# HGRN2 chain steps between projection matmuls: one step at each place, or two steps at every second place

## The chip, the cores and the metric

One core of a Trainium2 chip runs the kernel. The metric is device time in microseconds (us) of one execution. PE is TensorE (matmul), DVE is VectorE, ACT is ScalarE, POOL is GpSimd, SP issues the transfers.

## The reference, cut to what matters

One step of a streaming encoder with one layer. All 2048 new frames of a prompt (and 8 x 16 frames of running streams) go through one input projection to eight groups of 512 columns. Four of them (QA, KA, VA, GA) feed a stick-breaking attention with 8 heads, four (QH, FH, IH, GH) an HGRN2 recurrence with 4 heads of 128 x 128 state. An output projection and a layer norm follow. The change concerns the time in which the projection and the recurrence run together. The recurrence, per head:

```
f = lb + (1.0 - lb) * sigmoid(fh);  k = 1 - f;  q = silu(qh)
S_t = diag(f_t) S_{t-1} + k_t outer i_t
o_t = S_t^T q_t
o   = o * rsqrt(mean(o * o) + eps) * norm_g * silu(gh)
```

## The kernel before, in words

Everything is float32; projections are split in a high and a low part, so each product is three matmuls (lines 306 to 324). The order of the instructions is written out by hand: every engine runs its own instructions in the order in which the program issues them, and waits on semaphores where one needs another's result.

**Projection.** `order` (lines 222 to 231) lists the weight sections in two halves of the frames. In each half, head by head: IH (for two heads, ahead of heads 0 and 2), FH, QH, GH of the head, then 3, 3, 2 and 6 attention sections: KA0, QA0, VA0 after head 0; GA0, VA2, KA1 after head 1; QA1, GA1 after head 2; KA2, QA2, GA2, KA3, QA3, GA3 after head 3. A half has three tiles of tokens, of 384 columns (the last of the second half has 256; the last of the first half holds 256 prompt frames and the 128 frames of the running streams). For a narrow section a tile is one group of 24 matmuls into `pj` (`pe_T`, two buffers), with a gap after k = 2, after k = 5 and at its end, behind the evacuation (`evac_T`). VA and IH (wide sections) go by blocks of 128 tokens with two gaps per block (`pe_N`). At each gap `weave` is called (line 583). Evacuations: FH is a sigmoid on ACT (L337) and a tensor_scalar on DVE (L338); QH, GH and GA are a sigmoid on ACT (L327) and a product on DVE (L329, L331); QA, KA, VA are copies on ACT. After the first tile of a section (line 657) the next section's weights are split by `split_w`: casts on ACT (L107), subtractions on POOL (L115), two for a narrow section and four for a wide one.

**Recurrence.** After a head's GH section, its three tiles of tokens are appended to the list `chains` as three generators `hgrn` (line 393), which share the head's state. One call of `next` is one step. A chain has 14 steps:

- S (lines 405 to 412): kS = 1 - f, dp = q kS, q = q f, on DVE (L405, L411, L412); no matmul.
- seven levels 1, 2, 4, 8, 16, 32, 64 (lines 417 to 455): matmuls of kS and q into `ps` (two buffers): L418, six instructions, for levels 1 to 16; for levels 32 and 64 L431, with 32 or 64 columns into part of the output partitions. Then DVE rescales q (L443) and kS (L444), which the next level's matmuls read, keeps the scores (L435 or L438) and makes the next `tot` (L447). ACT and POOL make dh and dl at levels 2 and 4.
- K (lines 456 to 470): L457 and L458, the transposes of kS (L462), their copy kN on ACT (L464).
- U (471 to 486): pu = kN x i (L474), then the states on DVE (L484).
- O (487 to 501): po (L489, L491; L496 for the running streams), squares on ACT (L500).
- R (502 to 504): the reciprocal root on POOL (L129, L130).
- N (505 to 507): on = po x rs on DVE (L506), into a tile of one buffer.
- Q (508 to 516): transposes of `on` (L510), the gated product on DVE (L511), the store.

The third chain of a head in the first half holds the running streams and has two more steps: I, a product on POOL (L520), and B, its matmuls and state (L525, L527).

**The mixing.** `step_chain` (line 563) takes the first chain of the list, runs one step, and puts it back at the second place, so that the first two chains alternate and the third comes when one of them is done. `weave` adds the rate 1.0 to a credit, up to 2.0, and runs a step for each whole credit. `drain` (line 590) runs a chain to its end where a section needs its buffers.

Of the kernel before, what the change touches and what calls it, by code (L numbers as in the profile page):

```python
# [39 lines left out]
PASSES = ((0, 8), (8, 12), (12, 16))  # L40
NP = H // 2
HRATE = 1.0
SRATE = 0.9
CRATE = 2
ORATE = 0.9
# [20 lines left out]
def stream_step_kernel(ctx: ExitStack, tc: tile.TileContext, x_prompt, x_sample, cache_k, cache_v, state_s,  # L66
# [55 lines left out]
    def tick():  # L122
        for d in late:
            d[0] -= 1
        while late and late[0][0] <= 0:
            late.pop(0)[1]()
# [67 lines left out]
    with ExitStack() as ph:  # L194
# [366 lines left out]
        credit = [0.0]  # L561

        def step_chain():
            if not chains:
                return False
            g = chains.pop(0)
            done = next(g[1], 0) == 0
            if not done:
                chains.insert(min(1, len(chains)), g)
            return True  # L570

        RATE = HRATE

        prep = []

        def run_prep(n):
            while prep and n:
                if next(prep[0], 0) == 0:
                    prep.pop(0)
                else:  # L580
                    n -= 1

        def weave(rate):
            tick()
            run_prep(1)
            credit[0] = min(credit[0] + rate, 2.0)
            while credit[0] >= 1.0 and step_chain():
                credit[0] -= 1.0

        def drain(upto):  # L590
            while any(c[0] <= upto for c in chains):
# [18 lines left out]
        for i, (half, sec, j) in enumerate(order):  # L610
# [22 lines left out]
            for ti, (t0, n) in enumerate(TILES[half]):  # L633
                if wide(sec):
                    for b in range(n // P):
                        ps = pp.tile([P, 512], F32, name="pj", tag="pj")
                        o = ps[:, :256]
                        for _ in pe_N(ti, o, b, w):
                            weave(RATE)
                        evac_N(half, sec, j, ti, b, o, hg)  # L640
                        weave(RATE)
                else:
                    ps = pp.tile([P, 512], F32, name="pj", tag="pj")
                    o = ps[:, :n]
                    for _ in pe_T(ti, o, n, w):
                        weave(RATE)
                    if i == 1 and ti == 0:
                        next(consts, None)
                    for a in pend:
                        k_natural(*a)  # L650
                    pend = []
                    kn = evac_T(half, sec, j, ti, o, n, hg)
                    if kn:
                        pend.append(kn)
                    weave(RATE)
                if ti == (i == 0):
                    split_w(i + 1)
                elif ti == 1 and i + 2 < len(order):
                    load_raw(first_load[i + 2] + 2)
                if last:  # L660
                    prep.append(gen1(prep_x(1, ti)))
# [11 lines left out]
    with ExitStack() as ph:  # L673
# [318 lines left out]
        credit = [0.0]  # L992
# [7 lines left out]
        def run_steps(n0, n1, guest, rate):  # L1000
            for n in range(n0, n1):
                for fn in todo.pop(n, []):
                    fn()
                for i in range(2):
                    run_later()
                    s_part(n + LS, i)
                    if 0 <= n < NU:
                        t_part(n, i)
                    if i == 1:
                        z_part(n + LZ)  # L1010
                        c_part(n - 1)
                    tick()
                    if n >= -LZ:
                        credit[0] += rate
                    while credit[0] >= 1:
                        next(guest, None)
                        credit[0] -= 1
# [37 lines left out]
        credit[0] = C0  # L1055
        run_steps(0, NS, guest, SRATE)
        for _ in guest:
# [218 lines left out]
```

## Time and profile before

| what | value |
|---|---|
| runs of the kernel | median 1751.0 us of 3 (1747.85 to 1751.8) |
| the profiled execution | 1749.85 us |
| its span, first to last instruction | 1748.0 us |
| PE busy | 1707.1 us (98% of the span) |
| DVE, ACT, POOL busy | 958.5, 701.2, 731.2 us |
| the chain of work that ended last | 92% of it on PE |

The projections and the recurrence fill the first 990 us or so; attention, the running streams and the output projection follow. Rows of a timeline give the start and the duration in us, the engine, the line of the kernel, the operation, output<-inputs, shapes and how many instructions are merged (x6); in brackets the idle time before it and what ended it. Durations of matmuls reach into the next one: their ends are modelled.

### The profile page before, as it was taken

The numbers are of one execution on the slowest core, as the hardware profiler recorded it, in microseconds if no ns is written. First come the engines' busy times: TensorE is split into PE (matmuls) and PEld (weight loads), VectorE is DVE, ScalarE is ACT, GpSimd is POOL, SyncE is SP. The second block draws the span as 40 slices with busy tenths as digits, with TensorE's granted clock in tenths as the row PEclk, the third lists the DMA queues.
The fourth block names the chain that finished last, engine by engine and source line by source line (L and its number), as shares of the span: only waits on it lengthen the run. The fifth ranks groups of instructions, "written<-read, shape, count | busy, mean of one in ns | idle before, by whom it ended". The sixth has DMA issues, their size and how long they took to land.

```text
span 1748.0 us, 33628 instructions
## 1 busy us (share of the span) xinstructions
PE 1707.1 (98%) x12901; PEld 1464.1 (84%) x12901; DVE 958.5 (55%) x1762; ACT 701.2 (40%) x1593; POOL 731.2 (42%) x822
## 2 busy tenths in 40 slices
PE   8999999999999999999999999999999999999998
PEld 8999999999999999999999866666666667666886
DVE  4254543355443352642665367777877767666454
ACT  3221220212213222211222267777777877767210
POOL 1122321213221322221222266666766776766564
PEclk9999999999999999999999989999999999999999
DMA  4133232122244231231122476786644533131243
GB/s 166 53 89 102 63 100 61 48 63 62 81 120 135 62 103 56 80 90 40 61 62 76 124 189 159 176 187 152 152 113 136 185 114 102 53 114 40 92 147 115
DMA packets 288167, 180.01 MB, mean 103 GB/s; under 512 B 112636, under 2 KB 272904, under 8 KB 288008
## 3 DMA queue, kind: packets, MB, share of 16 engines
q1 hardware_dynamic: 288008, 177.86, 35.9%
q8 instruction: 103, 1.69, 0.4%
q14 instruction: 56, 0.46, 0.1%
HBM read 130.63 MB, written 47.71 MB: 102 GB/s over the span
## 4 chain that ended last, share of the span: by engine, by line
PE 92%; DVE 3%; ACT 1%; DMA 1%; issue 1%; SPq 1%; POOL 0%; POOLq 0%; DVEq 0%; ACTq 0%
PE pj L309 11%; PE pj L311 10%; PE pj L310 10%; PE z L734 9%; PE po L783 7%; PE wt L767 7%; PE py L1109 4%; PE ps L418 4%; PE pj L319 4%; PE pj L321 4%; PE pj L320 4%; PE py L1111 4%; PE py L1110 4%; PE pk L864 2%; PE so L945 1%; PE ps L431 1%
## 5 line engine op out<-in xcount | busy, mean ns | idle before, releaser
L115 POOL TENSOR_TENSOR wl<-wr,wh 128x512 fp32r<-128x512 f32 x126 | 163.8, 1322 | 578.7 <-ACT wh L107 561.0
L309 PE MATMUL pj<-xh,wh 128*128 128x384 f32 (+1 forms) x1152 | 395.5, 343 | 0.0
L754 POOL TENSOR_TENSOR s<-s,pr 128x512 f32<-128x512 f32 (+3 forms) x320 | 325.7, 1024 | 130.0 <-DVE pr L701 112.8
L311 PE MATMUL pj<-xh,wl 128*128 128x384 f32 (+1 forms) x1152 | 376.2, 327 | 0.0
L310 PE MATMUL pj<-xl,wh 128*128 128x384 f32 (+1 forms) x1152 | 375.8, 326 | 0.0
L701 DVE TENSOR_TENSOR_SCAN pr<-keep,pr,one 128x513 f32<-128x513 f32 x192 | 238.7, 1270 | 74.1 <-ACT keep L740 67.5
L309 PEld LDWEIGHTS pj<-xh,wh 128*128 128x128 f32 x1152 | 217.3, 189 | 2.7 <-issue 0.7
L310 PEld LDWEIGHTS pj<-xl,wh 128*128 128x128 f32 x1152 | 217.5, 189 | 0.7 <-issue 0.7
L311 PEld LDWEIGHTS pj<-xh,wl 128*128 128x128 f32 x1152 | 216.7, 188 | 0.0
L783 PEld LDWEIGHTS po<-wh,vst 128*64 128x64 f32 x2176 | 116.3, 137 | 100.6 <-issue 82.3
L737 ACT ACTIVATE s<-z 128x512 f32<-128x512 f32 (+3 forms) x320 | 173.4, 542 | 61.4 <-PE z L734 57.8
L107 ACT COPY wh<-wt 128x512 f32<-128x512 f32 (+3 forms) x320 | 165.6, 539 | 78.2 <-PE wt L767 65.1
L767 PE MATMUL wt<-ident,s 128*128 128x128 f32 x1088 | 171.5, 282 | 0.2
L734 PE MATMUL z<-kst,qr 64*128 64x512 f32 (+3 forms) x640 | 170.5, 587 | 0.1
L767 PEld LDWEIGHTS wt<-ident,s 128*128 128x128 f32 x1088 | 124.0, 142 | 45.2 <-issue 19.1
L319 PE MATMUL pj<-wh,xh 128*128 128x256 f32 x544 | 160.4, 295 | 0.0
L783 PE MATMUL po<-wh,vst 128*64 128x128 f32 x2176 | 155.0, 281 | 0.0
L320 PE MATMUL pj<-wl,xh 128*128 128x256 f32 x544 | 152.3, 280 | 0.3 <-POOL wl L115 0.3
L321 PE MATMUL pj<-wh,xl 128*128 128x256 f32 x544 | 152.2, 280 | 0.0
L327 ACT ACTIVATE sg<-pj 128x384 f32<-128x384 f32 (+1 forms) x72 | 34.1, 474 | 231.3 <-PE pj L311 217.9
L740 ACT ACTIVATE keep<-z 128x512 f32<-128x512 f32 (+2 forms) x230 | 126.0, 548 | 0.0
L701 DVE TENSOR_TENSOR_SCAN pr<-keep,one 128x385 f32<-128x385 f32 (+3 forms) x124 | 99.7, 820 | 33.2 <-ACT keep L740 17.6
(162 smaller groups left out, 2783.8 us busy)
## 6 DMA issues: line engine op xcount, KB each, us to landing
wr<-in_w_in SPq DMA_DIRECT2D x64, 512.0 KB
kr<-in_cache_k SPq DMA_DIRECT2D x16, 1024.0 KB
vr<-in_cache_v SPq DMA_DIRECT2D x32, 512.0 KB
mt<-mx_d SPq DMA_DIRECT2D x136, 64.0 KB
x<-in_x_prompt SPq DMA_DIRECT2D x16, 512.0 KB
kst<-kT_d SPq DMA_DIRECT2D x16, 512.0 KB
vst<-v_d SPq DMA_DIRECT2D x16, 512.0 KB
out<-xr SPq DMA_DIRECT2D x16, 512.0 KB
```

The source lines that it names most:

```text
L309: mm(o, wh[:, k], xh[:, k, :n], start=k == 0, stop=False)
L310: mm(o, wh[:, k], xl[:, k, :n], start=False, stop=False)
L311: mm(o, wl[:, k], xh[:, k, :n], start=False, stop=k == KT - 1)
L319: mm(o, xh[:, k, ts], wh[:, k], start=k == 0, stop=False)
L320: mm(o, xh[:, k, ts], wl[:, k], start=False, stop=False)
L321: mm(o, xl[:, k, ts], wh[:, k], start=False, stop=k == KT - 1)
L701: dve.tensor_tensor_scan(pr[:, CW - wd:CW + 1][:, ::-1], kr, by, carry, ALU.mult, ALU.bypass)
L734: mm(z[:, :wd], q[r, q0:q0 + P], k[r, lo:hi], start=not top, stop=True, skip_group_check=True)
L737: act.activation(s[:, :wd], z[:, :wd], AF.Sigmoid, scale=SC)
L754: pool.tensor_tensor(s[:, :wd], s[:, :wd], pr[:, CW - wd + 1:CW + 1], ALU.mult)
L767: nc.tensor.transpose(pt_[:, x:x + P], U[(u, a)][0][:, x:x + P], ident)
L783: mm(o[r, :P], v[:, lo // P + x, r], th[a][:, x * P:(x + 1) * P], start=top and x == 0, stop=bot and x == n - 1)
```

## The change

A constant HB = 2 is added. `weave` still counts a credit of 1.0 per call, now up to 4.0, and runs steps only when the credit has reached HB; then it runs as many as the credit pays for. Nothing else is changed.

```diff
+HB = 2
...
         def weave(rate):
             tick()
             run_prep(1)
-            credit[0] = min(credit[0] + rate, 2.0)
-            while credit[0] >= 1.0 and step_chain():
-                credit[0] -= 1.0
+            credit[0] = min(credit[0] + rate, 4.0)
+            if credit[0] >= HB:
+                while credit[0] >= 1.0 and step_chain():
+                    credit[0] -= 1.0
```

## Rows read from the trace of the kernel before

**Rows 1.** Windows: us, busy us (instructions) by engine, granted clock, DMA share, GB/s.
```profile
60.00:980.00 920.00, 908.09 (x6520) 885.58 (x6519) 417.81 (x1092) 197.19 (x514) 228.73 (x256) 1.00 0.26 76
```
**Rows 2.** Waits of PE, 60 to 980 us: total us, times, longest.
```profile
PE ps L418 <- DVE kS L444: 6.7, 9, 1.3
PE ps L418 <- DVE sc L435: 2.6, 2, 1.3
```
**Rows 3.** Timeline of PE, 253 to 264 us, two steps of one chain.
```profile
253.25 0.83 PE L418 MATMUL ps<-hq,kS 128*128 128x128 f32 x6
...
260.91 0.91 PE L418 MATMUL ps<-hq,kS 128*128 128x128 f32 x6 [1.30 <-DVE kS L444]
```
**Rows 4.** Timeline of DVE, the same stretch.
```profile
254.40 0.35 DVE L444 TENSOR_TENSOR kS<-kS,hf 128x192 f32<-128x192 f32 x1
...
259.35 1.42 DVE L444 TENSOR_TENSOR kS<-kS,tot 128x192 f32<-128x192 f32 x1
```
**Rows 5.** Timeline of PE, the end of GH of head 1.
```profile
195.07 0.33 PE L309 MATMUL pj<-xh,wh 128*128 128x384 f32 x1
...
197.15 0.33 PE L309 MATMUL pj<-xh,wh 128*128 128x384 f32 x1
```
**Rows 6.** Timeline of DVE, the two steps S that open head 1.
```profile
196.31 0.62 DVE L331 SCALAR_TENSOR_TENSOR hg<-pj,vecs,sg 128x384 f32<-128x384 f32 x1 [3.54 <-ACT sg L327]
...
...
197.83 0.56 DVE L412 TENSOR_TENSOR hq<-hq,hf 128x384 f32<-128x384 f32 x1
...
199.28 0.56 DVE L412 TENSOR_TENSOR hq<-hq,hf 128x384 f32<-128x384 f32 x1
```
**Rows 7.** Timeline of PE, a step of level 32.
```profile
105.41 0.47 PE L431 MATMUL ps<-hq,kS 128*32 128x32 f32 x12
```
**Rows 8.** Timeline of DVE, the same step.
```profile
106.18 0.35 DVE L444 TENSOR_TENSOR kS<-kS,tot 128x192 f32<-128x192 f32 x1
```
**Rows 9.** Timeline of PE, the transposes of a step K.
```profile
114.01 0.49 PE L462 MATMUL pk<-ident,kS 128*128 128x128 f32 x3
```
**Rows 10.** Timeline of ACT, the copy of the same step.
```profile
114.59 0.48 ACT L464 COPY kN<-pk 128x384 f32<-128x384 f32 x1 [2.47 <-PE pk L462]
```
**Rows 11.** Timeline of PE, the end of a step O with running streams.
```profile
157.43 1.95 PE L496 MATMUL po<-s,qz 128*128 128x128 f32 x16
```
**Rows 12.** Timeline of DVE, step N of the same chain.
```profile
161.56 0.56 DVE L506 TENSOR_TENSOR on<-po,rs 128x384 f32<-128x384 f32 x1
```
**Rows 13.** Timeline of ACT, the evacuation of an FH group.
```profile
314.19 0.49 ACT L337 ACTIVATE hf<-pj 128x384 f32<-128x384 f32 x1 [3.67 <-PE pj L311]
```
**Rows 14.** Timeline of DVE, the same evacuation.
```profile
314.72 0.48 DVE L338 TENSOR_SCALAR hf<-hf,oml,lb 128x384 f32<-128x384 f32 x1 [3.68 <-ACT hf L337]
```
**Rows 15.** Timeline of POOL, two weight splits and step I.
```profile
161.53 2.54 POOL L115 TENSOR_TENSOR wl<-wr,wh 128x512 fp32r<-128x512 f32 x2
164.03 1.90 POOL L520 TENSOR_TENSOR qz<-hi,hmask 128x1024 f32<-128x1024 f32 x1
```
**Rows 16.** Timeline of PE, step Q of the first of two chains.
```profile
132.69 0.49 PE L510 MATMUL pq<-ident,on 128*128 128x128 f32 x3
```
**Rows 17.** Timeline of DVE, step N of the second chain.
```profile
133.39 0.56 DVE L506 TENSOR_TENSOR on<-po,rs 128x384 f32<-128x384 f32 x1 [7.54 <-ACT vt L381]
```
**Rows 18.** Timeline of PE, a step of level 64 between projections.
```profile
111.22 0.34 PE L311 MATMUL pj<-xh,wl 128*128 128x384 f32 x1
111.49 0.56 PE L431 MATMUL ps<-hq,kS 128*64 128x64 f32 x6
...
112.27 0.34 PE L310 MATMUL pj<-xl,wh 128*128 128x384 f32 x1
```
**Rows 19.** Windows, granted clock in the seventh number group (columns as in rows 1).
```profile
530.00:540.00 10.00, 8.36 (x63) 8.08 (x62) 4.12 (x7) 2.89 (x6) 0.12 (x1) 1.00 0.83 277
...
1036.00:1038.00 2.00, 0.56 (x5) 0.56 (x6) 2.00 (x3) 0.00 (x0) 1.41 (x2) 1.00 0.73 223
1038.00:1042.00 4.00, 4.00 (x29) 3.38 (x28) 2.69 (x5) 1.81 (x6) 2.58 (x5) 0.61 1.07 277
```

## The prediction

> **What bounds the kernel now.** I read the windows over the projection stage first. From 60 to 980 us TensorE is busy 908.09 of 920.00 us at a granted clock of 1.00; DVE is busy 418, ACT 197, POOL 229 [rows 1]. The change reorders work in this stage alone, and here every microsecond in which TensorE waits is added to the end. Next the list of waits of TensorE: in the whole stage it waits 6.7 us in 9 cases for L444 and 2.6 us in 2 for L435, both of the chains' steps on DVE [rows 2]. So the chains are hidden almost completely, and the reason is their spacing: the reader is to see that the waits are few and not longer than 1.3 us. Last I read the timeline at single places, for what a step needs from the one ahead of it.
>
> **Recurrence of a chain.** A level step's six matmuls start at 253.25 [rows 3]. DVE then rescales q (L443) and kS (L444, from 254.40 for 0.35 us) [rows 4], so the result stands at 254.75. From the end of an L444 to the matmuls that waited for it goes 0.14 us: 259.35 + 1.42 = 260.77, start 260.91 [rows 3, 4]. The next level of the same chain can thus start 254.89 - 253.25 = 1.64 us after the first. The six matmuls themselves hold TensorE 0.67 us (0.83 shown, of which the following matmul overlaps 0.16). Two levels of one chain behind each other leave TensorE idle 0.97 us, and the group after a wait took 0.91 instead of 0.83 [rows 3]: **1.05 us**. In the kernel before a third of a projection group, six or nine matmuls (1.04 to 1.56 us at 0.173, below), always stands between, which is why it is nearly free.
>
> **What the change does to the order.** I followed the list `chains` through all 568 weaves. Steps stay 344, in the same order, and none is left for a drain. Before, 336 places hold steps, one each (8 hold two). After, there are 164: 96 hold one step of each of two chains, 8 hold four, and **60 hold two steps of the same chain**. `step_chain` alternates among the first two chains, but each head has three, so the third runs alone, and its two steps lie behind each other with no projection between.
>
> **The terms**, for eight head groups (four heads, two halves):
>
> 1. *Opening, 8 groups.* The list is empty when a head's chains arrive, so the credit stands at its cap: 2 before (S, S), 4 now (S, S, 1, 1). The first place is at 197.15, nine projection matmuls after the head's last group ended; twelve take 2.08 us from 195.07, so 0.173 each [rows 5]. On DVE the gate evacuation (L331) ends at 196.93, the first S (its last operation is L412) at 197.83 + 0.56 = 198.39, the second at 199.84 [rows 6]. The first level step could start at 198.53 instead of 197.15 (wait 1.38), end at 199.20, and the second at 199.98 (wait 0.78). 2.2 us each: **+17.6**.
> 2. *Pairs (2, 4) and (8, 16) of the third chain*, 16 places; some have two blocks of tokens and less work, so 1.0: **+16**. In six of the eight (8, 16) the weight splits (L115 on POOL) run beside it and L443 or L444 takes 1.42 instead of 0.35 [rows 4]: one or two such, 8.6 more; but before waits there already (most of the 9.3 in rows 2, I take 6.5): **+2**.
> 3. *(32, 64)*, 8 places: level 32 starts at 105.41 and shows 0.47, so it holds TensorE to about 105.75 [rows 7]; L444 ends at 106.53 [rows 8]; plus 0.14: 0.95 us, and twice the two stand behind an evacuation on DVE (0.65): **+9**.
> 4. *(K, U)*, 8 places: the transposes start at 114.01 and hold TensorE to 114.34 [rows 9], the copy of kN on ACT ends at 115.07 [rows 10], plus 0.14: 0.87, with the slow start 0.95: **+7.6**.
> 5. *(O, R)*: R is on POOL alone, nothing. *(N, Q)*, 8 places: from the last matmul of O (157.43 + 1.95 - 0.16 = 159.22 [rows 11]) to the end of N (161.56 + 0.56 [rows 12]) and on to Q go 3.0 us; two weaves cover 2.6 to 2.8. 0.3 in five cases. In three the place is the end of a group, and N queues behind its evacuation, which ends on DVE 1.2 us after the last matmul [rows 13, 14]; then 0.56, 0.14 and the slow start: 2.0. **+7.5**.
> 6. *(S, 1)* of the third chain: in heads 2 and 3 of both halves it stands at the end of a group (FH or GA), where S queues on DVE behind the evacuation. ACT starts 0.2 us after the last matmul (314.19 [rows 13]), L338 ends at 315.20 [rows 14], S takes 1.46 (196.93 to 198.39 [rows 6]): 315.20 + 1.46 + 0.14 less 313.99 is 2.8, with the slow start 2.9 us of waiting, and an estimated 2.45 in the second half, where the third chain has two blocks for three: **+10.7**. Elsewhere DVE runs S ahead: nothing.
> 7. *(I, B)*, four places. I is 1.90 us on POOL, behind two splits of 2.54 us [rows 15] that begin some 1.3 us after a section's first tile, so it ends 5.7 us after it. B stands 3.9 us after that tile in head 3 (wait 1.9) and, since term 5 has held TensorE, 5.4 in heads 0 and 2 (wait 0.4 each); in head 1 no split is near. **+2.7**.
> 8. *(Q, Q) of the first two chains*, 8 places: `on` has one buffer, so the second N waits for the first Q (132.69 to 133.39), runs 0.56 to 133.95 [rows 16, 17], and the second Q can start at 134.09, when TensorE has been free since 133.02: 1.07. Before, a weave lay between. **+9**.
> 9. *Two chains under the splits*. DVE now gets two steps at once. Where four splits stand (ahead of a wide section, 1.3 to 6.5 us after the tile), two operations of 1.42 for each chain [rows 4] let the second chain's next matmuls start some 7.1 us after the tile; they are due at 5.1, so 2.0 us, where the kernel before waited up to 1.3 [rows 2]: 0.7 in head 1, and 1.4 at level 64 in head 0, in both halves. **+4**, between 0, if the splits fall between the steps, and 14, if every group's first two sections are hit.
> 10. *What is won.* Levels 32 and 64 write part of the output partitions, and from the projection ahead (111.22) to the second behind (112.27) go 1.05 us [rows 18]; two projections are 0.35, six matmuls 0.40 (0.56 shown less 0.23, over five gaps, is 0.066 each). 0.30 us is the change of shape. 24 such places fall away: **-7**. Around ordinary steps the same sum leaves 0.006 us: nothing.
>
> Sum: 17.6 + 16 + 2 + 9 + 7.6 + 7.5 + 10.7 + 2.7 + 9 + 4 - 7 = **+79 us**. Against the profiled execution's 1749.85 us that is 1829; the median of the runs stands 1.15 higher, so I say **1830**. At nothing I cost the half of the steps that come one weave later, with their stores (SP) and the load of the state, which is needed five places, or ten weaves, later; dl on POOL has three places; and the projection's evacuations that stand behind a waiting N on DVE, since `pj` has two buffers. If those covers fail, evacuations are late and TensorE waits at the next group.
>
> **The clock.** It stayed at 1.00 over 530 to 540 with TensorE busy 8.36 of 10 us, but after a stretch with 0.56 busy of 2.00 it fell to the lower level, 1.2 GHz, for most of the next 4 us, whose mean is 0.61 [rows 19]; that costs 0.39 x 4 = 1.6 us. The waits of terms 2 and 6 that reach 2.5 to 3 us could do the same.
>
> **Rivals.**
> - *The clock falls* at some eight of the long waits: 8 x 1.6 = 13 more, **1843**. For it: rows 19; against: the stage before kept 1.00 throughout, and dense projections follow each wait at once. The Trainium skill, TensorE: Matmul & The Clock Gate (Why this matters for your kernels), asks for no idle gaps between bursts of matmuls, as the array falls back to half its clock; by that rule this case would be the likelier. The trace bears it out only for a stretch nearly empty.
> - *It does what its words say*, always one step of each chain: terms 1, 8, 9 and 10 stay, +24, **1774**. The list with three chains speaks against it.
> - *Faster*: DVE, ACT and POOL are idle half of the stage, and if they had every next step ready, only term 10 were left: 1749.85 - 7, **1743**. It decides if a pair costs under 7 / 156 = 0.045 us per place. Against it stand 1.64 us of recurrence and in-order waiting [rows 2, 3].
> - *No change*: as many waits as term 10 gives back, at some seven places alone, 1751; it needs the same readiness as the case before.
>
> **How the numbers follow.** Forecast 0.73, clock 0.16, words 0.04, faster 0.04, no change 0.03. Low bounds of the terms (opening 13, pairs of 2 at 14 and -2, 6, 6.5, 4, 8, 0, 7, 0, -7) sum to about 49, so 1799; high ones (20, 18, 8, 11, 9, 12, 13, 8, 10, 10, -5) to 114, which with everything high at once is too much; I take 1857, which holds most of the clock's case. A measurement here tells 0.2% (3.5 us) from no change: faster 0.04, same 0.03, slower 0.93.
>
> **What would show it.** In the changed trace: TensorE's waits in the stage near 90 us instead of 10, in some 60 to 70 cases; at third-chain places two L418 groups 1.6 us apart with L444 as releaser; a wait for L412 at each head's opening; a wait of L510 for L506 of about 1 us; kN by ACT ahead of L474. The busy times of DVE, ACT and POOL stay. I am wrong if the third chain's level steps follow without a wait, or if the waits come but the stage after ends as early as now.

## The result, and the profile after

The changed kernel takes **1831.85 us** in the median of 4 runs (1829.49 to 1837.48), the kernel before 1749.42 us in 4 runs on the same chip (1747.16 to 1751.8). The ratio is 1.0474, 95% interval 1.0453 to 1.0495: slower by 82 us. The forecast said 1830, in 1799 to 1857.

The profiled run took 1837.48 us, its span 1835.6 us. The engines' busy times on the page of the changed kernel:

```profile
PE 1731.1 (94%) x12901; PEld 1482.1 (81%) x12901; DVE 950.3 (52%) x1762; ACT 701.4 (38%) x1593; POOL 730.9 (40%) x822
```

The work is the same (12901 matmuls, and DVE, ACT and POOL within 8.2 us of before); TensorE's busy time has grown by 24 us. Some 11 of it is the model of matmul ends (a matmul with a wait behind it is shown 0.16 us longer than it holds TensorE, and there are some 70 waits); the rest, some 13 us, fits the slower clock shown below. The last projection matmul ends at 994.0 us before and at 1078.9 us now, +84.9 us; what follows it took 754.0 us and now 756.7, with the clock at its lower level for 6.8 us more. So nearly all of the loss is in the projection stage, as the prediction had it. (1.9 us of the 84.9 stand ahead of it: in the profiled run the first matmul of L310 starts at 45.0 us, its counterpart L309 before at 43.1.) The windows of the changed kernel over that stage:

```profile
60.00:1065.00 1005.00, 930.11 (x6532) 901.81 (x6531) 409.93 (x1092) 197.67 (x515) 227.61 (x256) 0.98 0.24 70
```

Beside [rows 1], TensorE is busy 930 us instead of 908, for 12 matmuls more, and is idle 75 instead of 12; the clock's mean is 0.98 instead of 1.00. Two things, then: waits, and a clock. First the waits of PE in the changed kernel, from 60 to 1070 us:

```profile
PE ps L419 <- DVE hq L413: 21.7, 20, 2.6
PE ps L419 <- DVE kS L445: 19.0, 16, 2.0
PE pq L511 <- DVE on L507: 11.2, 11, 1.8
PE ps L432 <- DVE kS L445: 7.0, 8, 1.4
PE pu L475 <- ACT kN L465: 4.1, 8, 0.6
PE ps L458 <- DVE tot L448: 3.3, 2, 1.8
PE ps L419 <- DVE sc L436: 3.1, 2, 1.6
PE pb L526 <- POOL qz L521: 2.6, 2, 2.4
...
PE ps L419 <- DVE tot L448: 1.0, 4, 0.4
```

(The numbers of lines behind the inserted constant are one or two higher.) Where [rows 2] had 9.3 us in 11 cases, there are 73 us in 73. The four largest kinds of releaser are the prediction's: L413 for S, L445 for the chain's own rescaling, L507 for N, L465 for kN. One place of each kind shows the size. Two levels of a third chain, timelines of PE and of DVE in the changed kernel:

```profile
146.32 0.83 PE L419 MATMUL ps<-hq,kS 128*128 128x128 f32 x6
147.96 0.91 PE L419 MATMUL ps<-hq,kS 128*128 128x128 f32 x6 [0.81 <-DVE kS L445]
```

```profile
147.19 0.36 DVE L444 TENSOR_TENSOR hq<-hq,tot 128x192 f32<-128x192 f32 x1 [2.03 <-PE ps L419]
147.46 0.35 DVE L445 TENSOR_TENSOR kS<-kS,tot 128x192 f32<-128x192 f32 x1
```

The two groups start 1.64 us apart, as worked out ahead. The opening of head 0, PE and DVE of the changed kernel:

```profile
85.65 0.93 PE L419 MATMUL ps<-hq,kS 128*128 128x128 f32 x6 [1.12 <-DVE hq L413]
87.10 0.94 PE L419 MATMUL ps<-hq,kS 128*128 128x128 f32 x6 [0.52 <-DVE hq L413]
```

```profile
85.04 0.56 DVE L413 TENSOR_TENSOR hq<-hq,hf 128x384 f32<-128x384 f32 x1
...
86.49 0.56 DVE L413 TENSOR_TENSOR hq<-hq,hf 128x384 f32<-128x384 f32 x1
```

L413 ends at 85.60 and its matmuls start 0.05 us later; the prediction had allowed 0.14. The pair (Q, Q), PE of the changed kernel:

```profile
138.40 0.49 PE L511 MATMUL pq<-ident,on 128*128 128x128 f32 x3
139.71 0.55 PE L511 MATMUL pq<-ident,on 128*128 128x128 f32 x3 [0.82 <-DVE on L507]
```

The second Q waits for a normalisation that could not begin until the first Q had read the one buffer.

Then the clock. The place (S, 1) of head 2, first half, in windows and in the timeline of PE of the changed kernel:

```profile
414.00:419.00 5.00, 2.78 (x17) 2.46 (x15) 2.47 (x6) 0.77 (x2) 0.00 (x0) 1.00 0.63 184
419.00:423.00 4.00, 3.67 (x14) 3.67 (x15) 1.64 (x5) 0.23 (x1) 1.00 (x1) 0.57 0.00 0
423.00:427.00 4.00, 3.19 (x23) 3.03 (x22) 1.26 (x4) 0.00 (x0) 0.00 (x0) 1.00 0.00 0
...
526.00:532.00 6.00, 5.11 (x33) 4.95 (x34) 2.55 (x9) 0.00 (x0) 1.00 (x1) 1.00 0.03 8
```

```profile
419.33 1.65 PE L419 MATMUL ps<-hq,kS 128*128 128x128 f32 x6 [2.55 <-DVE hq L413]
```

After 5 us with TensorE busy 2.78, the clock falls to its lower level, 1.2 GHz, for most of 4 us: the six matmuls that take 0.83 us elsewhere take 1.65. The stage has nine such stretches, 30.7 us together, and had none before. At half the clock they cost up to 15.4 us. Eight follow waits for the chains, of 1.75 to 2.55 us or two behind each other (1.12 and 0.52 at least); the ninth follows a wait of 1.81 us for a load (L301, at 589.86). The length of the wait does not decide alone: behind the longest of all, 2.62 us up to 526.08, the clock stays at 1.00 (last row). Why the wait ahead of it is 2.55 us long is seen on DVE, in the timeline of the same place:

```profile
417.34 0.48 DVE L339 TENSOR_SCALAR hf<-hf,oml,lb 128x384 f32<-128x384 f32 x1 [2.46 <-ACT hf L338]
...
418.72 0.56 DVE L413 TENSOR_TENSOR hq<-hq,hf 128x384 f32<-128x384 f32 x1
```

The group's evacuation (L339) stands ahead of step S, whose last operation (L413) ends at 419.28.

### The profile page after: what moved, and what is told of

Its sections match the earlier page's. It is cut to its first block, busy times and chain, and to the rows that moved or that the text cites. A ratio compares the mean times of both kernels' runs of the same rounds, so it can differ in the third digit from the quotient of the medians.

```text
span 1835.6 us, 33633 instructions
## 1 busy us (share of the span) xinstructions
PE 1731.1 (94%) x12901; PEld 1482.1 (81%) x12901; DVE 950.3 (52%) x1762; ACT 701.4 (38%) x1593; POOL 730.9 (40%) x822
## 4 chain that ended last, share of the span: by engine, by line
PE 62%; DVE 3%; ACT 1%; issue 1%; DMA 1%; POOL 0%; SPq 0%; POOLq 0%; DVEq 0%; ACTq 0%
PE z L736 8%; PE po L785 7%; PE wt L769 7%; PE pj L310 5%; PE pj L312 5%; PE pj L311 5%; PE py L1111 4%; PE py L1113 3%; PE py L1112 3%; PE ps L419 2%; PE pk L866 2%; PE pj L320 2%; PE pj L322 2%; PE pj L321 2%; PE so L947 1%
## 5 line engine op out<-in xcount | busy, mean ns | idle before, releaser
L310 PE MATMUL pj<-xh,wh 128*128 128x384 f32 (+1 forms) x1152 | 393.7, 342 | 0.0
L116 POOL TENSOR_TENSOR wl<-wr,wh 128x512 fp32r<-128x512 f32 x126 | 163.4, 1319 | 558.8 <-ACT wh L108 558.8
L311 PE MATMUL pj<-xl,wh 128*128 128x384 f32 (+1 forms) x1152 | 380.6, 330 | 0.0
L312 PE MATMUL pj<-xh,wl 128*128 128x384 f32 (+1 forms) x1152 | 380.4, 330 | 0.0
L310 PEld LDWEIGHTS pj<-xh,wh 128*128 128x128 f32 x1152 | 221.2, 192 | 1.8 <-issue 0.7
L311 PEld LDWEIGHTS pj<-xl,wh 128*128 128x128 f32 x1152 | 221.2, 192 | 0.7 <-issue 0.7
L312 PEld LDWEIGHTS pj<-xh,wl 128*128 128x128 f32 x1152 | 220.6, 191 | 0.0
L419 PE MATMUL ps<-hq,kS 128*128 128x128 f32 x672 | 95.5, 283 | 44.8 <-DVE hq L413 21.7
L419 PEld LDWEIGHTS ps<-hq,kS 128*128 128x128 f32 x672 | 85.5, 193 | 53.7 <-DVE hq L413 22.2
```

What stands on the lines that cost most here:

```text
L310: mm(o, wh[:, k], xh[:, k, :n], start=k == 0, stop=False)
L311: mm(o, wh[:, k], xl[:, k, :n], start=False, stop=False)
L312: mm(o, wl[:, k], xh[:, k, :n], start=False, stop=k == KT - 1)
L419: mm(ps[:, c], ch(kS, c), ch(q, c), start=True, stop=True)
```

## The experiments

Theory: the waits that the prediction lists, at the places where two steps of one chain stand together or DVE has only just been given the step ahead, and on top a clock that falls after some of them. For a sum that doesn't depend on how often the clock fell, I take each run's time by its mean granted clock, "us at full clock", and average it over the runs. It is an estimate (not everything in the span follows that clock): 1740 before, 1807 after, so **+67 for waits, net of what the change saves, and the other 15 of the 82 for the clock**.

**e1_cap2: the opening's credit as before.**

```diff
-            credit[0] = min(credit[0] + rate, 4.0)
+            credit[0] = min(credit[0] + rate, 2.0)
```

> The changed kernel with the credit's cap at 2 again: the opening place of each head holds S, S alone, and levels 1, 1 come two weaves later. Theory (the time is the sum of in-order waits of TensorE): the 16 opening waits for L412 go, which the trace of the changed kernel shows as 8 pairs of 1.40 to 1.77 us, 12.4 us idle and some 0.16 us more each for the modelled overlap, 15 us in all: 1817 us (1812 to 1821). Rival (the third chain alone makes the time, an opening wait only moves later ones): 1830 to 1833.

Measured: 1807.11 us in 4 runs, ratio to the kernel before 1.0326 (1.0294 to 1.0358): 24.7 us less than the changed kernel, below the range that was expected. Waits of PE in this kernel, from 60 us to the end of the stage:

```profile
PE ps L419 <- DVE kS L445: 20.5, 16, 2.7
PE ps L419 <- DVE sc L436: 8.6, 8, 2.3
PE ps L432 <- DVE sc L439: 7.1, 7, 2.3
PE pq L511 <- DVE on L507: 6.9, 9, 1.2
```

All waits for L413 are gone, 21.7 us in 20 cases, and 12.4 us in 16 of these were the opening's. The other four are (S, 1) of the third chain: with S, S alone at the opening, every later step stands one place on, and the third chain's S is no longer at the end of a group (on DVE it comes behind a product of Q, L512, and not behind an evacuation); the three long waits of (N, Q) went the same way. In exchange 15.7 us of waits for the two `ps` buffers stand (L436, L439), 3.1 before. So terms 5 and 6 are not properties of the pairing, but of which place falls on a group's end.

**e2_third1: the third chain, alone in the list, one step at a place.**

```diff
-            if credit[0] >= HB:
+            if credit[0] >= (HB if len(chains) > 1 else 1):
```

> The changed kernel, but with one step at every weave while a single chain is left: the places of two chains stay paired. Theory (the 60 places with two steps of one chain carry most of the loss): their waits, some 55 us with overlap in the changed trace, go, about 8 us of them come back as in the kernel before, and some 5 to 10 us of fallen clock go with them: 1775 us (1766 to 1788). Rival (pairing itself costs, DVE gets two steps at once and the projections' evacuations are late): 1805 to 1832.

Measured: 1783.66 us, ratio 1.0197 (1.0175 to 1.0218). The theory holds: without the third chain's pairs 48 of the 82 us are gone, some 37 of them waits and 11 clock by the estimate (1770 us at full clock). This kernel is also the rival "it does what its words say", priced at 1774; the missing 10 us are partly a wait that it did not have. Waits of PE in this kernel:

```profile
PE ps L419 <- DVE hq L413: 12.6, 17, 1.2
PE pb L526 <- POOL qz L521: 6.7, 3, 2.5
PE pq L511 <- DVE on L507: 6.4, 8, 1.2
PE ps L419 <- DVE kS L445: 3.8, 7, 1.2
```

The openings and (Q, Q) remain whole, and B of the running streams now comes upon POOL's product three times.

**e4_third2: the kernel before, with the third chain alone in pairs.**

```diff
-            while credit[0] >= 1.0 and step_chain():
-                credit[0] -= 1.0
+            if credit[0] >= (HB if len(chains) == 1 else 1):
+                while credit[0] >= 1.0 and step_chain():
+                    credit[0] -= 1.0
```

> The kernel before with only the third chain paired: one step at each weave while two or three chains are left, two at every second weave when one is left; the cap stays 2. Theory: the third chain's waits alone, 55 us less 8 of before, and 5 to 10 us of fallen clock: 1749 + 55 = 1804 us (1792 to 1815). Rival (pairing two chains is what costs): 1750 to 1775.

Measured: 1783.96 us, ratio 1.02 (1.0178 to 1.0222): between the two expectations, in neither. Waits of PE in this kernel:

```profile
PE ps L419 <- DVE kS L445: 20.4, 16, 2.7
PE ps L432 <- DVE kS L445: 5.6, 8, 0.7
PE pu L475 <- ACT kN L465: 4.1, 8, 0.6
PE ps L419 <- DVE sc L436: 2.6, 2, 1.3
```

The level pairs and (K, U) are there nearly in full; the waits for L413 and the long ones for L507 are not. The expectation had counted terms 5 and 6, which need the changed kernel's places, as e1 shows. Without them this is the price of the third chain's pairs by themselves: about 34 us, 28 of it waits by the estimate.

**e3_on2: two buffers for the normalised output.**

```diff
-            on = hw.tile([P, 3, P], F32, name="on", tag="on", bufs=1)
+            on = hw.tile([P, 3, P], F32, name="on", tag="on", bufs=2)
```

> The changed kernel with two buffers for the tile on. Theory: the second N no longer waits for the first Q, and the 8 waits of 0.71 to 0.82 us between two L510 groups go, 7.4 us with overlap: 1824 us (1821 to 1828). Rival (N waits for R on POOL, or the time returns at the next evacuation): 1831 to 1833.

Measured: 1829.76 us, 1818.15 to 1833.09, ratio 1.0449 (1.0409 to 1.0489). By the time alone this is inconclusive. The trace is not: of the waits for L507 three are left, and the eight (Q, Q) are gone:

```profile
PE pq L511 <- DVE on L507: 5.1, 3, 1.8
```

At full clock it is 1801.6 us, 5.9 less than the changed kernel (1807.5 over its eight runs, those of e6 with them), near the 6.1 us of waits that went. What spreads the times is the clock: the run of 1818.15 us had a mean of 0.991, the one of 1833.09 us 0.982.

**e5_fill and e6_after_again: the same waits, with and without matmuls in them.** In e5 matmuls whose result nobody reads are put ahead of the waiting level steps: 12 at level 1 of the third chain in heads 2 and 3, 3 or 6 at the openings, 4 at levels 4 and 16 of third chains, 10 at six of these. They are extra work, into a tile that the step then overwrites. e6 is the changed kernel, without an edit, on the same chip.

```diff
-            def scores(k):
+            def scores(k, fill=0):
                 ps = psc.tile([P, 4, P], F32, name="ps", tag="ps")
+                for _ in range(fill):
+                    mm(ps[:, :3], ones, xT[0][0][:, 0], start=True, stop=True)
...
-                    ps = scores(k)
+                    ps = scores(k, fill)
```

> The changed kernel with matmuls that nobody reads put ahead of the level steps that wait (12 ahead of level 1 of the third chain in heads 2 and 3, 6 and 3 ahead of the two level steps that open a head, 4 ahead of levels 4 and 16 of the third chain, 10 at the six of these that the weight splits lengthen); each is 0.17 us of TensorE and their sum at a place is below the wait measured there, so that TensorE works in a time in which it waited. Their output is overwritten. Theory A (part of the loss is the clock that falls after waits, nine falls of 3.4 us in the stage's trace, up to 1.7 us each): six to eight of the falls go, the granted clock of the run rises from 0.983 to 0.987 towards 0.992, and the time falls by 8 to 14 us against the changed kernel in the same call: 1818 to 1824. Theory B (the waits alone, the clock costs nothing that counts): unchanged, 1830 to 1835.

> The changed kernel once more, beside the one with filled waits on the same chip: 1829 to 1837 us at a granted clock of 0.982 to 0.989; by theory A the runs with the lower clock are the longer ones, 1.8 us for each 0.001 (0.001 of 1832 us), by theory B clock and time do not go together.

Measured: e5 1817.69 us in 4 runs (1816.47 to 1819.95), ratio 1.0385 (1.0365 to 1.0404); e6 1832.3 us (1829.48 to 1834.73), ratio 1.0466 (1.0445 to 1.0487). **With 220 matmuls more the kernel is 14.6 us faster**, 0.3 us past the range of theory A. The runs of e6 order by their clock, as that theory asks: 1829.48 and 1830.35 us at 0.988, 1834.25 and 1834.73 at 0.986 and 0.985. The timeline of PE of e5 at the place shown above (in this kernel L419 is the added matmul and L421 the level step):

```profile
409.17 2.28 PE L419 MATMUL ps<-xh,ones 128*128 128x384 f32 x12
...
411.88 0.94 PE L421 MATMUL ps<-hq,kS 128*128 128x128 f32 x6 [0.42 <-DVE hq L413]
```

The windows of the stage in e5, and then in e6:

```profile
60.00:1047.00 987.00, 951.49 (x6741) 920.49 (x6740) 410.00 (x1092) 197.90 (x515) 228.07 (x256) 1.00 0.25 71
```

```profile
60.00:1058.00 998.00, 922.90 (x6525) 893.69 (x6524) 409.86 (x1092) 197.96 (x515) 227.64 (x256) 0.99 0.24 70
```

The real step starts no earlier relative to DVE (0.06 us behind L413, 0.05 above), but takes 0.94 us and not 1.65, and the clock never leaves its upper level in the stage; in e6 it falls six times, up to 10.2 us of cost, and the stage ends 10.9 us later than in e5. At full clock e5 is 1806 and e6 1808 us: the time of the steps is equal within 2 us, and the difference is the clock's. In e5 the last projection matmul ends at 1060.9 us, 66.9 after that of the kernel before: the price of the waits once more.

**e7_shape: term 10 by itself.** In the kernel before, levels 32 and 64 of the first two chains are put at one place, with no other pair.

```diff
-                yield
+                yield 2 if m >= BLK else 1
...
-            while credit[0] >= 1.0 and step_chain():
+            while credit[0] >= 1.0 and (v := step_chain()):
                 credit[0] -= 1.0
+                if v == 2 and len(chains) > 2:
+                    step_chain()
+                    credit[0] -= 1.0
```

> The kernel before, with only levels 32 and 64 of the first two chains put at one place (16 places fewer that change the shape of the output). Theory: 0.30 us for each, 16 x 0.30 = 4.8 us, less some waits of the second chain where weight splits stand: 1745 to 1749, ratio 0.997 to 1.000. Rival (the second chain's scores wait for a buffer of ps, as levels 64 do at up to 2.3 us in the trace with the cap at 2): 1750 to 1758.

Measured: 1749.24 us in 12 runs, the kernel before 1751.33 in 17, ratio 0.9993 (0.9982 to 1.0003): not told from no change. In the traces the stage ends 1.6 us earlier (992.45 for 994.01), although PE now waits for a free `ps`:

```profile
PE ps L431 <- DVE sc L438: 3.3, 5, 0.7
```

The two add up to 4.9 us, which fits 16 changes of shape at the 0.30 each of the prediction, with two thirds of it lost to that wait; one trace of each kernel is all that this rests on.

**e8_all3: everything that helped.** The changed kernel with the edits of e1, e2 and e3 together.

```diff
+            on = hw.tile([P, 3, P], F32, name="on", tag="on", bufs=2)
...
+            credit[0] = min(credit[0] + rate, 2.0)
+            if credit[0] >= (HB if len(chains) > 1 else 1):
```

> The changed kernel with the cap at 2, one step at each weave for a single chain, and two buffers for on: two chains stay paired. Theory (waits, read from the trace with cap 2): 16 us of waits for the buffers of ps at the paired places, 8 us at the third chain as in the kernel before, 3 us of clock, less 5 us of saved shape changes: 1767 us (1760 to 1773). Rival (pairing costs nothing once the third chain, the cap and on are cured): 1743 to 1752, and it beats both kernels.

Measured: 1764.66 us in 5 runs, ratio 1.008 (1.0063 to 1.0097). The waits of PE in this kernel say what is left:

```profile
PE ps L419 <- DVE sc L436: 8.7, 8, 2.3
PE ps L432 <- DVE sc L439: 7.1, 7, 2.3
PE ps L419 <- DVE kS L445: 6.8, 9, 1.3
```

Pure pairs of two different chains still lose 14 us, some 9 of it waits by the estimate (1749 us at full clock). In 15 places the second chain's matmuls wait, 15.8 us, for a `ps` buffer that DVE has not read yet: both chains need one in the same place, and there are two. At some of these places DVE is late itself: ahead of the wait of 2.3 us that ends at 212.70, L444 and L445 take 1.41 to 1.45 us, where 0.35 is usual, while POOL splits weights (L116). In e2, where the same pairs stand one place earlier, only 3.1 us in 2 cases were such waits. So the price depends on the place too; more buffers were not tried. No version here is faster than the kernel before by more than the noise.

## Why the prediction was right, point by point

The forecast of 1830 met 1831.85, but **by two errors that cancel**: the waits were put at +79 and cost +67, and the clock, put at nothing, cost +15. Term by term (idle time in the trace of the changed kernel, and 0.16 us for each wait, by which the last matmul ahead of it is shown too long; the value of term 10 is taken over from the prediction):

| term | predicted | measured |
|---|---|---|
| 1 opening | 17.6 | 15.0 (12.4 idle, 16 waits) |
| 2 pairs (2, 4), (8, 16), net | 18 | 12.5 (21.6 less some 9 that stood before) |
| 3 (32, 64) | 9 | 8.3 |
| 4 (K, U) | 7.6 | 5.4 |
| 5 (N, Q) | 7.5 | 5.6 |
| 6 (S, 1) | 10.7 | 9.9 (2.55, 2.62, 2.04, 2.05 idle) |
| 7 (I, B) | 2.7 | 3.1 |
| 8 (Q, Q) | 9 | 7.4 |
| 9 two chains under the splits | 4 | 5.4 |
| 10 shape | -7 | -7 by 0.30 a place, which e7 fits |
| sum | 79 | 66 |

- **What held.** That 60 of the pairs are two steps of one chain, and that these are the larger part: e2 returns 48 of 82 us. The 1.64 us of recurrence, to the hundredth. The places and the releasers, and nearly the count of waits ("60 to 70", 73 in the trace) and their sum ("near 90 us", 73 listed and 85 with the 0.16 for each). The busy times of DVE, ACT and POOL.
- **Terms 1, 4, 5 and 8 were over-sized in their small parts.** The hand-over of 0.14 us was read off one row behind L444 [rows 4] and used everywhere, but behind L413 it is 0.05, behind L465 0.05 (161.79 + 0.48 to 162.32) and behind the L507 of (Q, Q) 0.06 (139.09 + 0.56 to 139.71). Term 3's own rows give 0.92 us, where it says 0.95. The five small waits of 0.3 us in term 5 do not exist; its three long ones do, at 1.65 to 1.79 of idle time.
- **Term 2 took too little for what was there before**: 6.5 us of the waits in [rows 2], where about 9 turned into waits of the pairs.
- **The "slow start" of 0.08 us is real, and the table leaves it out.** PE of the kernel before, the second projection matmul behind each of the two level steps of [rows 3]:

```profile
254.09 0.34 PE L310 MATMUL pj<-xl,wh 128*128 128x384 f32 x1
...
261.83 0.34 PE L310 MATMUL pj<-xl,wh 128*128 128x384 f32 x1
```

From the start of the step that did not wait (253.25) to it go 0.84 us, from that of the step that did (260.91) 0.92. For some 60 waits more than before that is an estimated 5 us, and the sum would be about 71, against 67 by the clock and 66.9 in e5. Which term takes the difference of 4 us was not found.

- **The step that failed is the clock.** The forecast held it at 1.00, on the ground that dense projections follow each wait. They follow, but the trace shows that this does not keep the clock up: 2.78 us of 5 busy, and it fell. The rival "the clock falls" had the size right, eight falls and 13 us against nine (six in e6) and 15, and a chance of only 0.16; with the waits as the forecast had them it would have given 1843. The Trainium skill, TensorE: Matmul & The Clock Gate (Why this matters for your kernels), asks that bursts of matmuls have no long idle gaps between them, or the array goes back to its lower clock. The traces agree in the direction, since with the gaps ahead of the level steps filled in e5 nothing falls in the stage and 14.6 us come back; but the single waits ahead of the falls, at most 2.55 us, are shorter than the gaps that it warns of.
- **Words** (1774) is e2, at 1783.66: under-priced by 10. **Faster** (1743) asked for chains that are always ready; e7 fits the saving on which it stood, and waits for buffers take most of it back. **No change** (1751) asked for waits at some seven places; there are 73.

## What to carry to other kernels

Small steps of a dependent chain hide between dense matmuls by their spacing: put two of one chain together and the engine waits for the round trip through the other engine (here 0.97 us at a level step of three blocks), and put two of different chains together and they need two buffers at once, for which they may wait (15.8 us in e8). Before batching, write down which chain each step of a pair belongs to, since a rule that alternates between two of three lists leaves the third to follow itself. And when waits are added to a matmul engine, price the clock too, and compare runs by time and granted clock together: here three runs in four of one kernel said "no change" while 6 us of waits had gone.

## What the runs showed of the hardware that was not expected

- The clock of TensorE fell to 1.2 GHz in a stage that is shown 93% busy (930 of 1005 us), after waits of 1.1 to 2.6 us; not after all of them (nine falls, 73 waits, and none behind the longest), and not equally often in each run (six falls in e6, the same kernel). The mean granted clock of one kernel went from 0.982 to 0.991, and its time by 14.9 us with it (e3).
- Matmuls whose result nobody reads, put into waits, made a kernel 14.6 us faster (e5 beside e6).
- A shift of every step by one place moved waits of 15 us or so in and out (e1, e4): at the end of a group DVE has the evacuation (L339 or L330) ahead of the step, elsewhere it has run ahead.
